# Conditioning products issued eight at a time in every fourth step, not four in every second

## The chip, the cores and the metric

The kernel runs on one core of one Trainium2 chip. The metric is the device time of one launch in microseconds. Before the change, three runs gave a median of 3303.23 us (3293.81 to 3304.52). One further execution was recorded by the profiler; it took 3296.7 us, of which 3294.9 us lie between its first and its last instruction. All durations below come from that execution.

## The reference

One inference step of a two-layer model on 256 prompt rows and 8 x 4 sample rows (288 columns in the kernel). Each layer has a mixer and a gated convolutional FFN, and each of them is modulated by six vectors that come from a small conditioning matrix:

```python
cond = jax.nn.silu(c.astype(F32)).astype(x.dtype)          # 9 rows: 8 samples and the prompt
for layer in range(DEPTH):                                 # 2
    mod = (cond @ p['w_ada'][layer] + p['b_ada'][layer])[:, None, :]
    sh1, sc1, g1, sh2, sc2, g2 = jnp.split(mod, 6, axis=-1)
    h = _rms(x, p['g_mix'][layer]) * (1 + sc1) + sh1
    y, ... = _mixer_ab(h, ...)   # or _mixer_cd in layer 1
    x = x + g1 * y
    h = _rms(x, p['g_ffn'][layer]) * (1 + sc2) + sh2
    y, fb = _conv_ffn(h, ...)
    x = x + g2 * y
```

`w_ada` is 2048 x 12288 in each layer, so each of the twelve vectors costs one product of 9 rows with a 2048 x 2048 float32 matrix (16 MB).

## The kernel before

**The large products.** `project` multiplies the activations with one weight matrix. It takes the weights in tiles of 128 x 1024 floats (512 KB, four blocks of 128 rows by 256 columns). `weights` loads one such tile (`raw`, line 175, on SyncE's queue), makes its rounded part `whi` on ScalarE (line 179) and the rest `wlo` on VectorE (line 180), and TensorE then runs 24 matrix products on it: for each of 8 blocks one on line 206 (`whi` with the high part of the activations), one on 207 and one on 208 (`wlo`). One weight tile with its 24 products is called a step here; there are 768 steps in the program.

**The conditioning products.** Two of the twelve vectors are made in the start phase by `ada_quarter`. The other ten are made by `ada_steps`, a generator that is advanced in the background: `Ctx.step`, called at the head of `weights`, resumes it once per step in both mixers (`every` is 1), about once in 1.9 steps in the first FFN and once in 2 steps in the second. It loads `w_ada` in tiles of the same size (`araw`, 128 rows by 1024 columns) and multiplies them with `cond` in `ada_groups` (line 1890). One block of 128 rows of `w_ada` needs two `araw` tiles and four products, which go to four different strips of 32 PSUM partitions. They are called a group of four here. The profile counts each of these float32 products as two instructions, so a group of four appears as x8.

**Buffers.** `raw` and `araw` share one pool of five buffers, `whi` and `wlo` have three each:

```python
class Ctx:
    raw_bufs, hl_bufs, kb = 5, 3, 4
    c.wraw = ctx.enter_context(tc.tile_pool(name="wraw", bufs=c.raw_bufs))
    c.whl = ctx.enter_context(tc.tile_pool(name="whl", bufs=c.hl_bufs))
```

A `raw` buffer is free again when VectorE has made `wlo`; an `araw` buffer when TensorE has run its two products. All `raw` and `araw` loads go through SyncE's queue in the order of the program, so a load that waits for its buffer holds up those behind it. The framework orders the instructions of each engine and gives out the buffers when the program is built; both are fixed in the built program.

Of the kernel before, what the change touches and what calls it, by code (L numbers as in the profile page):

```python
# [9 lines left out]
F32 = mybir.dt.float32  # L10
# [5 lines left out]
P = 128  # L16
# [5 lines left out]
D = 2048  # L22
KT = D // P
# [5 lines left out]
def bc(ap, axis, n):  # L29

    a = ap.unsqueeze(axis)
    s = list(a.shape)
    s[axis] = n
    return a.to_broadcast(s)
# [79 lines left out]
def mtile(c, name="pm"):  # L114
    return c.pm.tile([P, 512], F32, tag="pm", name=name)


def transpose(c, out, in_):
    n = in_.shape[0]
    b = in_.base_partition() if callable(getattr(in_, "base_partition", None)) else 0  # L120
    c.nc.tensor.transpose(out, in_, c.ident[:n, :n])  # L121
# [1765 lines left out]
def ada_groups(c, ps, cond, pieces, ks, first, last):  # L1887

    for r in range(4):
        c.nc.tensor.matmul(ps[32 * r:32 * r + 32, :], cond[:, ks[r], :], pieces[r], start=first, stop=last)  # L1890


def ada_steps(c, cond, w, which, bias, mod):

    nc = c.nc
    ps = c.pa.tile([P, 512], F32, tag="pa", name="pa")
    for k in range(KT):
        pieces = []
        for h in range(2):
            raw = c.wraw.tile([P, 1024], F32, tag="raw", name="araw")  # L1900
            nc.sync.dma_start(raw, w[k * P:(k + 1) * P, which * D + h * 1024:which * D + (h + 1) * 1024])
            pieces += [raw[:, 0:512], raw[:, 512:1024]]
            if h:
                ada_groups(c, ps, cond, pieces, [k] * 4, k == 0, k == KT - 1)
            yield
    pt = mtile(c)
    for t in range(0, 4, 2):
        sb = c.misc.tile([P, T], F32, tag="tmp", name="adas", bufs=2)[:, :2 * P]
        nc.scalar.copy(sb, ps[:, t * P:(t + 2) * P])
        for j in range(2):  # L1910
            transpose(c, pt[:, (t + j) * P:(t + j + 1) * P], sb[:, j * P:(j + 1) * P])
    pv = pt.rearrange("p (t j s) -> p j t s", t=4, j=4)
    mv = mod.rearrange("p (j t) s -> p j t s", t=4)
    bv = bias.rearrange("p (j t) -> p j t", t=4)
    for t in range(4):
        nc.vector.tensor_tensor(mv[:, :, t], pv[:, :, t, 0:9], bc(bv[:, :, t], 2, 9), ALU.add)
    yield
# [322 lines left out]
def trunk(tc, I, O):  # L2240
    nc = tc.nc
    with ExitStack() as ctx:
# [42 lines left out]
        with tc.tile_pool(name="start", bufs=1, side="right") as st:  # L2285
# [31 lines left out]
            for k in range(0, KT, 2):  # L2317
                act.scale(k)
            pr.place(c, slice(0, 1))
            ada = lambda l, i: ada_steps(c, cond, I["w_ada"][l], i, pr("b_ada%d" % l)[:, 16 * i:16 * i + 16], mods[l][:, i])  # L2320

            def quarter(q):
# [110 lines left out]
```

## Time and profile before

| what | value |
|---|---|
| median of three runs | 3303.23 us |
| the profiled execution, its span | 3296.7 us, 3294.9 us |
| TensorE busy with products | 3191.8 us, 97% |
| VectorE, ScalarE, GpSimd busy | 2060.3, 1451.5, 419.6 us |
| loads of `araw` and `raw` | 384 and 768, 512 KB each |
| conditioning products on line 1890 | 1536 instructions, 275.3 us |
| mean granted TensorE clock | 0.985 of full speed |

TensorE is busy nearly throughout, and the products overlap in its pipeline, so the busy times of single products (about 300 ns) are longer than the distance between their starts. What a piece of TensorE's work costs is read from start to start.

### The profile page before, as it was taken

Reading aid. Unit: us, or ns where it says so; the run is one execution under the profiler, and the core shown is the slowest. Engines: PE = TensorE matmul, PEld = TensorE weight load, DVE = VectorE, ACT = ScalarE, POOL = GpSimd, SP = SyncE. Lnnn points to the kernel's source line nnn. Section 1 sums busy time; section 2 is a strip of 40 time slices with the busy share of each in tenths; the row PEclk is TensorE's granted clock in tenths of the full one; section 3 lists DMA queues with packets and bytes.
Section 4 is the critical chain, followed back from the end, with each engine's and each line's share of the span. In section 5 each row is a group of like instructions: output and inputs, shape, how many; then the busy total and the mean of one; then the engine's idle time right before and its main releaser. Section 6 shows DMA issues by size and latency. Waiting matters only on the chain.

```text
span 3294.9 us, 58934 instructions
## 1 busy us (share of the span) xinstructions
PE 3191.8 (97%) x23220; PEld 2844.7 (86%) x23220; DVE 2060.3 (63%) x4291; ACT 1451.5 (44%) x2277; POOL 419.6 (13%) x786
## 2 busy tenths in 40 slices
PE   7899999999999999999999999999999999999998
PEld 3478888888889999999999977877889999999997
DVE  4255566676787566667656776666775556565566
ACT  1133343343554434343434675444464435444353
POOL 2000011110231101010001210112131101010020
PEclk9999999999999999999999999999999999999999
DMA  8866654545677777777777655665467755555553
GB/s 290 266 203 231 217 187 151 161 156 187 183 217 227 227 237 239 234 238 251 238 239 232 197 186 185 223 214 163 149 198 229 227 164 167 167 165 165 164 173 109
DMA packets 506615, 663.80 MB, mean 201 GB/s; under 512 B 42409, under 2 KB 436453, under 8 KB 506329
## 3 DMA queue, kind: packets, MB, share of 16 engines
q1 hardware_dynamic: 470930, 610.68, 58.5%
q0 software_dynamic: 14272, 40.76, 4.1%
q10 hardware_dynamic: 21136, 8.61, 1.0%
q8 instruction: 182, 2.98, 0.4%
q14 instruction: 95, 0.78, 0.1%
HBM read 634.13 MB, written 25.79 MB: 200 GB/s over the span
## 4 chain that ended last, share of the span: by engine, by line
PE 81%; DMA 9%; DVE 5%; ACT 3%; issue 2%; POOL 0%; SPq 0%; ACTq 0%; DVEq 0%; POOLq 0%
PE pp L206 22%; PE pp L208 22%; PE pp L207 22%; PE pa L1890 6%; DMA raw<-in_w_in_ab 3%; DVE wlo L180 2%; DMA araw<-in_w_ada 2%; DMA raw<-in_w_in_cd 2%; PE pm L121 1%; ACT whi L179 1%; PE pm L1100 1%; PE pm L1096 1%; PE pm L1104 1%; PE pm L1049 0%; PE pm L1827 0%
## 5 line engine op out<-in xcount | busy, mean ns | idle before, releaser
L206 PE MATMUL pp<-hhi,whi 128*128 128x288 f32 (+1 forms) x4736 | 1428.1, 302 | 6.9 <-ACT whi L179 3.3
L208 PE MATMUL pp<-hhi,wlo 128*128 128x288 f32 (+1 forms) x4736 | 1420.4, 300 | 8.8 <-DVE wlo L180 8.6
L207 PE MATMUL pp<-hlo,whi 128*128 128x288 f32 (+1 forms) x4736 | 1416.8, 299 | 0.1
L180 DVE TENSOR_TENSOR wlo<-raw,whi 128x1024 fp32r<-128x1024 f32 x768 | 943.3, 1229 | 753.3 <-ACT whi L179 737.7
L179 ACT CAST whi<-raw 128x1024 fp32r<-128x1024 f32 x768 | 805.4, 1049 | 1250.7 <-PE pp L207 723.7
L206 PEld LDWEIGHTS pp<-hhi,whi 128*128 128x128 f32 x4736 | 900.5, 190 | 138.8 <-issue 88.9
L208 PEld LDWEIGHTS pp<-hhi,wlo 128*128 128x128 f32 x4736 | 900.1, 190 | 35.3 <-DVE wlo L180 16.7
L207 PEld LDWEIGHTS pp<-hlo,whi 128*128 128x128 f32 x4736 | 899.8, 190 | 19.4 <-issue 15.5
L206 PE MATMUL pp<-hh,whi 128*128 128x288 f32 x1408 | 417.2, 296 | 0.0
L208 PE MATMUL pp<-hh,wlo 128*128 128x288 f32 x1408 | 416.7, 296 | 0.0
L207 PE MATMUL pp<-hl,whi 128*128 128x288 f32 x1408 | 413.5, 294 | 0.0
L1890 PE MATMUL pa<-araw,cond 128*32 128x512 f32 x1536 | 275.3, 612 | 21.7 <-DMA araw<-in_w_ada 21.7
L206 PEld LDWEIGHTS pp<-hh,whi 128*128 128x128 f32 x1408 | 264.7, 188 | 15.1 <-issue 13.4
L207 PEld LDWEIGHTS pp<-hl,whi 128*128 128x128 f32 x1408 | 266.6, 189 | 0.0
L208 PEld LDWEIGHTS pp<-hh,wlo 128*128 128x128 f32 x1408 | 264.2, 188 | 0.1
L507 DVE SCALAR_TENSOR_TENSOR cv<-pad,params,cv 128x304 f32<-128x304 f32 (+1 forms) x460 | 224.8, 532 | 20.1 <-ACT cv L505 11.8
L500 POOL COPY ffnpo<-pad 128x4 f32<-128x4 f32 x88 | 64.6, 734 | 1222.0 <-ACT pad L497 1222.0
L406 DVE SCALAR_TENSOR_TENSOR x<-pp,mod,x 128x256 f32<-128x256 f32 x256 | 112.4, 478 | 81.8 <-PE pp L208 80.8
L505 ACT ACTIVATE cv<-pad,params 128x304 f32<-128x304 f32 (+1 forms) x212 | 125.4, 637 | 7.8 <-DVE s_phi L1657 0.4
L1890 PEld LDWEIGHTS pa<-araw,cond 128*32 128x32 f32 x1536 | 39.7, 108 | 79.1 <-issue 40.4
L496 POOL COPY pad<-ffnsi 128x32 f32<-128x32 f32 x88 | 82.6, 938 | 18.1 <-ACT ffnsi L445 17.7
L497 ACT COPY pad<-pp 128x512 f32<-128x512 f32 x102 | 59.2, 581 | 12.9 <-PE pp L208 12.8
(785 smaller groups left out, 2618.0 us busy)
## 6 DMA issues: line engine op xcount, KB each, us to landing
araw<-in_w_ada SPq DMA_DIRECT2D x384, 512.0 KB, 4.8
raw<-in_w_ffn_up SPq DMA_DIRECT2D x352, 512.0 KB, 3.7
raw<-in_w_ffn_down SPq DMA_DIRECT2D x176, 512.0 KB, 3.5
raw<-in_w_in_ab SPq DMA_DIRECT2D x112, 512.0 KB, 4.9
raw<-in_w_in_cd SPq DMA_DIRECT2D x56, 512.0 KB, 5.1
raw<-in_w_out_ab SPq DMA_DIRECT2D x32, 512.0 KB, 5.5
raw<-in_w_out_cd SPq DMA_DIRECT2D x32, 512.0 KB, 3.6
s5d<-5p_D ACTq DMA_DIRECT2D x8, 838.0 KB, 5.6
```

The source lines that it names most:

```text
L179: nc.scalar.copy(hi[:, :n], raw[:, :n])
L180: nc.vector.tensor_tensor(lo[:, :n], raw[:, :n], hi[:, :n].bitcast(F32), ALU.subtract)
L206: nc.tensor.matmul(o, hi[:, k, js], ah, start=(k0 + k == first), stop=False)
L207: nc.tensor.matmul(o, hi[:, k, js], al, start=False, stop=False)
L208: nc.tensor.matmul(o, lo[:, k, js], ah, start=False, stop=(k0 + k == last))
L406: nc.vector.scalar_tensor_tensor(x[:, k + j, :SEQ], y[:, j, :SEQ], g[:, k + j, 8:9], x[:, k + j, :SEQ], ALU.mult, ALU.add)
L496: nc.gpsimd.tensor_copy(pv[:, :, :, 0:n], sv)
L497: nc.scalar.copy(pad[:, :, n:n + SEQ], ps[:, :, :SEQ])
L500: nc.gpsimd.tensor_copy(po[:, :, t0:t0 + 2], pad[:, :, SEQ:SEQ + n].rearrange("p j r -> p r j"))
L505: nc.scalar.activation(a, pad[:, j, 0:L], AF.Identity, scale=w(0), bias=pr(bname, t0 + j))
L507: nc.vector.scalar_tensor_tensor(a, pad[:, j, i:i + L], w(i), a, ALU.mult, ALU.add)
L1890: c.nc.tensor.matmul(ps[32 * r:32 * r + 32, :], cond[:, ks[r], :], pieces[r], start=first, stop=last)
```

## The change

`ada_steps` still gives way as many times, but it works in one resume out of four: it then loads four `araw` tiles (two blocks of 128 rows) one after the other and issues the eight products of both blocks together. Before, each resume loaded one tile, and every second one also issued four products. The number of loads and products is the same.

```diff
     ps = c.pa.tile([P, 512], F32, tag="pa", name="pa")
-    for k in range(KT):
+    for k0 in range(0, KT, 2):
+        for _ in range(3):
+            yield
         pieces = []
-        for h in range(2):
-            raw = c.wraw.tile([P, 1024], F32, tag="raw", name="araw")
-            nc.sync.dma_start(raw, w[k * P:(k + 1) * P, which * D + h * 1024:which * D + (h + 1) * 1024])
-            pieces += [raw[:, 0:512], raw[:, 512:1024]]
-            if h:
-                ada_groups(c, ps, cond, pieces, [k] * 4, k == 0, k == KT - 1)
-            yield
+        for k in (k0, k0 + 1):
+            for h in range(2):
+                raw = c.wraw.tile([P, 1024], F32, tag="raw", name="araw")
+                nc.sync.dma_start(raw, w[k * P:(k + 1) * P, which * D + h * 1024:which * D + (h + 1) * 1024])
+                pieces += [raw[:, 0:512], raw[:, 512:1024]]
+        for k in (k0, k0 + 1):
+            ada_groups(c, ps, cond, pieces[4 * (k - k0):4 * (k - k0) + 4], [k] * 4, k == 0, k == KT - 1)
+        yield
     pt = mtile(c)
```

In the built program TensorE's products of line 1890 stand in 229 unbroken runs before and in 153 now; of the latter 61 hold all eight products, the others are cut by small products of the mixers or belong to the start phase, which is the same in both.

TensorE in the first FFN, before: one run between two steps (`araw` is a tile of `w_ada`, `pp` the sum of a large product).

```order
L208 MATMUL pp_11506<-hh_8802,wlo_11552 128x288
L1890 MATMUL pa_11361<-araw_11507,cond_99 32x512 x2
L1890 MATMUL pa_11361<-araw_11585,cond_99 32x512 x2
L206 MATMUL pp_11584<-hh_8802,whi_11603 128x288
L207 MATMUL pp_11584<-hl_8803,whi_11603 128x288
```

The same place now:

```order
L208 MATMUL pp_11498<-hh_8802,wlo_11542 128x288
L1890 MATMUL pa_11361<-araw_11575,cond_99 32x512 x2
L1890 MATMUL pa_11361<-araw_11577,cond_99 32x512 x2
L1890 MATMUL pa_11361<-araw_11579,cond_99 32x512 x2
L1890 MATMUL pa_11361<-araw_11581,cond_99 32x512 x2
L206 MATMUL pp_11574<-hh_8802,whi_11603 128x288
```

Eight products stand together, and the next run of this kind comes seven or eight steps later, not four.

SyncE's queue at that place, before (a load that waits for `DVE` takes over the buffer of a weight tile, one that waits for `PE` that of a tile of `w_ada`; `DMAHW` are earlier loads):

```order
L1901 DMA araw_11507<-in_w_ada 128x1024 [waits DMAHW1_49,DVE_49]
L175 DMA raw_11509<-in_w_ffn_down 128x4x256 [waits DMAHW3_49,DVE_49]
L175 DMA raw_11549<-in_w_ffn_down 128x4x256 [waits DMAHW4_49,DVE_49]
L1901 DMA araw_11585<-in_w_ada 128x1024 [waits DMAHW0_49,PE_49]
L175 DMA raw_11601<-in_w_ffn_down 128x4x256 [waits DMAHW2_49,PE_49]
L175 DMA raw_11631<-in_w_ffn_down 128x4x256 [waits DMAHW6_49,DVE_49]
```

Now:

```order
L175 DMA raw_11539<-in_w_ffn_down 128x4x256 [waits DMAHW7_49,DVE_49]
L1904 DMA araw_11575<-in_w_ada 128x1024 [waits DMAHW0_49,DVE_49]
L1904 DMA araw_11577<-in_w_ada 128x1024 [waits DMAHW1_49,DVE_49]
L1904 DMA araw_11579<-in_w_ada 128x1024 [waits DMAHW2_49,DVE_49]
L1904 DMA araw_11581<-in_w_ada 128x1024 [waits DMAHW3_49,DVE_49]
L175 DMA raw_11601<-in_w_ffn_down 128x4x256 [waits DMAHW4_49,DVE_49]
L175 DMA raw_11631<-in_w_ffn_down 128x4x256 [waits DMAHW1_49,DVE_49]
L175 DMA raw_11677<-in_w_ffn_down 128x4x256 [waits DMAHW5_49,PE_49]
L175 DMA raw_11713<-in_w_ffn_down 128x4x256 [waits DMAHW6_49,PE_49]
L175 DMA raw_11749<-in_w_ffn_down 128x4x256 [waits DMAHW7_49,PE_49]
L175 DMA raw_11792<-in_w_ffn_down 128x4x256 [waits DMAHW0_49,PE_49]
```

The four `araw` tiles take four of the five buffers until their products have run. By the addresses in the built program, `raw_11601` takes over the buffer of `raw_11539`, the last weight tile ahead of the run of eight, and `raw_11631` takes over that of `raw_11601`.

SyncE's queue in the first mixer, where every step resumes `ada_steps`, now (before, one `araw` stood ahead of every `raw`):

```order
L1904 DMA araw_2478<-in_w_ada 128x1024 [waits DMAHW3_49,PE_49]
L1904 DMA araw_2480<-in_w_ada 128x1024 [waits DMAHW4_49,PE_49]
L1904 DMA araw_2482<-in_w_ada 128x1024 [waits DMAHW6_49,DVE_49]
L1904 DMA araw_2484<-in_w_ada 128x1024 [waits DMAHW7_49,DVE_49]
L175 DMA raw_2494<-in_w_in_ab 128x4x256 [waits DMAHW0_49,DVE_49]
L175 DMA raw_2537<-in_w_in_ab 128x4x256 [waits DMAHW5_49,DVE_49]
L175 DMA raw_2568<-in_w_in_ab 128x4x256 [waits DMAHW1_49,PE_49]
L175 DMA raw_2600<-in_w_in_ab 128x4x256 [waits DMAHW2_49,PE_49]
```

Here, too, `raw_2537` takes over the buffer of `raw_2494`, the load just ahead of it.

## Rows read from the trace of the kernel before

**Rows 1.** The page: busy time and share of the span by engine, the granted clock.

```profile
PE 3191.8 (97%) x23220; PEld 2844.7 (86%) x23220; DVE 2060.3 (63%) x4291; ACT 1451.5 (44%) x2277; POOL 419.6 (13%) x786
...
PEclk9999999999999999999999999999999999999999
```

**Rows 2.** The page: the chain that ended last, by engine.

```profile
PE 81%; DMA 9%; DVE 5%; ACT 3%; issue 2%; POOL 0%; SPq 0%; ACTq 0%; DVEq 0%; POOLq 0%
```

**Rows 3.** Timeline, one group of four in the first FFN: start us, us, engine.

```profile
1309.96 0.29 PE L208 MATMUL pp<-hhi,wlo 128*128 128x288 f32 x1
1310.18 0.16 PEld L1890 LDWEIGHTS pa<-araw,cond 128*32 128x32 f32 x8 [0.17 <-issue]
1310.19 1.06 PE L1890 MATMUL pa<-araw,cond 128*32 128x512 f32 x8
1311.18 0.40 PE L206 MATMUL pp<-hhi,whi 128*128 128x288 f32 x1
1311.42 0.29 PE L207 MATMUL pp<-hlo,whi 128*128 128x288 f32 x1
1311.55 0.29 PE L208 MATMUL pp<-hhi,wlo 128*128 128x288 f32 x1
...
1324.17 1.07 PE L1890 MATMUL pa<-araw,cond 128*32 128x512 f32 x8
```

**Rows 4.** Timeline, TensorE in the second mixer: five products in one run.

```profile
2187.59 0.29 PE L207 MATMUL pp<-hlo,whi 128*128 128x288 f32 x1
2187.82 1.90 PE L1890 MATMUL pa<-araw,cond 128*32 128x512 f32 x10
2189.65 1.13 PE L1424 MATMUL pm<-s_xw,s_Bt 128*128 128x512 f32 x2
```

**Rows 5.** Timeline, VectorE, SyncE's queue and ScalarE: from one buffer's release to its next.

```profile
1294.67 1.23 DVE L180 TENSOR_TENSOR wlo<-raw,whi 128x1024 fp32r<-128x1024 f32 x1 [1.12 <-ACT whi L179]
...
1295.93 0.37 SPq L175 DMA_DIRECT2D raw<-in_w_ffn_up  x1
...
1299.53 1.05 ACT L179 CAST whi<-raw 128x1024 fp32r<-128x1024 f32 x1 [3.18 <-DMA raw<-in_w_ffn_up]
...
1300.61 1.22 DVE L180 TENSOR_TENSOR wlo<-raw,whi 128x1024 fp32r<-128x1024 f32 x1 [3.01 <-ACT whi L179]
```

**Rows 6.** The same, where other ScalarE and VectorE work stands between.

```profile
1268.37 0.37 SPq L175 DMA_DIRECT2D raw<-in_w_ffn_up  x1
...
1272.06 1.05 ACT L179 CAST whi<-raw 128x1024 fp32r<-128x1024 f32 x1 [2.82 <-DVE cm_u L1507]
...
1273.77 1.22 DVE L180 TENSOR_TENSOR wlo<-raw,whi 128x1024 fp32r<-128x1024 f32 x1
```

**Rows 7.** Groups of line 179, second FFN without conditioning loads (2630:2900): busy, mean | idle, releaser.

```profile
L179 ACT CAST whi<-raw 128x1024 fp32r<-128x1024 f32 x84 | 88.4, 1052 | 136.2 <-PE pp L207 136.2
```

**Rows 8.** The same group in the first FFN (1150:1500).

```profile
L179 ACT CAST whi<-raw 128x1024 fp32r<-128x1024 f32 x99 | 103.7, 1048 | 176.4 <-PE pp L207 80.8 <-DMA raw<-in_w_ffn_up 56.2 <-DMA raw<-in_w_ffn_down 19.4
```

**Rows 9.** The same group in the first mixer (274:360).

```profile
L179 ACT CAST whi<-raw 128x1024 fp32r<-128x1024 f32 x21 | 22.0, 1049 | 54.0 <-DMA raw<-in_w_in_ab 54.0
```

**Rows 10.** Timeline, TensorE in the first mixer: starts of three groups of four (first halves).

```profile
275.38 0.64 PE L1890 MATMUL pa<-araw,cond 128*32 128x512 f32 x4
...
282.98 0.64 PE L1890 MATMUL pa<-araw,cond 128*32 128x512 f32 x4
...
290.54 0.64 PE L1890 MATMUL pa<-araw,cond 128*32 128x512 f32 x4
```

**Rows 11.** Stretches: us, busy (instructions) by engine, PEclk, DMA share and GB/s.

```profile
92.00:104.00 12.00, 10.35 (x49) 4.65 (x46) 2.07 (x6) 1.59 (x3) 0.00 (x0) 1.00 0.95 322
274.00:360.00 86.00, 83.80 (x621) 71.13 (x621) 33.15 (x44) 25.92 (x33) 3.58 (x6) 1.00 0.79 262
1150.00:1500.00 350.00, 349.78 (x2611) 324.40 (x2610) 236.58 (x570) 146.35 (x200) 32.30 (x68) 1.00 0.76 240
```

**Rows 12.** Weight loads of line 175 in 2630:2900, issue to landing.

```profile
DMA to landing us min/median/max: 3.3/3.6/5.5
```

**Rows 13.** The page: the groups of lines 206 and 208 in the large products.

```profile
L206 PE MATMUL pp<-hhi,whi 128*128 128x288 f32 (+1 forms) x4736 | 1428.1, 302 | 6.9 <-ACT whi L179 3.3
L208 PE MATMUL pp<-hhi,wlo 128*128 128x288 f32 (+1 forms) x4736 | 1420.4, 300 | 8.8 <-DVE wlo L180 8.6
```

## The prediction

> **What bounds the kernel now.** I read the page first. TensorE is busy for 97% of the span at nearly the full granted clock [rows 1], and 81% of the chain that ended last is TensorE's own work, with 9% DMA behind it [rows 2]. So there are two things to look for: what the change takes off TensorE's own time, and whether it makes weights arrive later than TensorE wants them.
>
> Next comes the price of a group of four, from start to start [rows 3]. The last large product ahead of it starts at 1309.96, the first one behind it at 1311.18, so 1.22 us pass. A plain step from one large product to the next is 0.13 us (1311.42 to 1311.55), and the first step behind the group takes 0.24. The group thus costs 1.22 + 0.24 - 2 x 0.13 = 1.20 us. The next group starts 13.98 us later [rows 3]; less 1.20 that leaves four steps of 3.20 us each, 24 products at 0.133. Nothing waits there.
>
> The third view is the way of one weight tile. Where a load waits for a buffer, it is issued at once when `wlo` of the old tile is done: VectorE ends at 1295.90, the load goes out at 1295.93, ScalarE starts at 1299.53, VectorE ends at 1301.83 [rows 5]. I call this a link: 5.9 us from issue to release. With other work in the way it took 6.6 us, from 1268.37 to 1274.99 [rows 6]. The load alone is about 3.6 us of it [rows 12], cast, subtraction and handing over 2.4 us.
>
> How early is a tile ready? In the second FFN without conditioning loads every idle time of line 179 ends with TensorE [rows 7]: the cast waits for one of three `whi` buffers, so it starts when TensorE is through with the tile three before. That is two steps, 6.4 us, ahead of its own use; 2.4 us later its `raw` buffer is free, **4.0 us ahead of its use**. In the first FFN 81 of 176 us idle end that way and 76 us with a load [rows 8]; in the first mixer all 54 us end with a load [rows 9]. So the lead is thinner where conditioning loads run, and thinnest in the mixers.
>
> **What the change takes away.** Two groups of four become one run of eight. The profile holds a run longer than four: five products (x10), where the fifth starts a second round on the strips [rows 4]. From the product ahead to the one behind it 2.06 us pass (2187.59 to 2189.65). A second round thus adds 2.06 - 1.20 = 0.86 us, not another 1.20; what is saved is one entry and one exit, 0.34 us. Built, the runs fall from 229 to 153, so 76 x 0.34 = **26 us** (0.8%) at most, all on TensorE, which is the bound.
>
> Here the Trainium skill speaks against the change. "TensorE: Matmul & The Clock Gate", section "Part 3: Packing small matmuls", says that weight loads overlap products in flight only when they use another group of rows. All products here use all rows, so by that rule the second four would wait for the first four to drain and nothing would be saved. The rows say otherwise: eight loads (two for each product) are over at 1310.34, while the products run to 1311.25 [rows 3], and the fifth product of [rows 4] did not cost another 1.20. I follow the rows.
>
> **What it adds: weights behind one buffer.** Instructions, bytes and resumes are the same. What moves is that four `araw` tiles now hold four of five buffers until their products have run, and the weight tiles behind them share what is left. By the built order the first two weight tiles behind the four loads go through one buffer, one after the other, and the rest wait in SyncE's queue behind the second of them.
>
> First FFN, 32 such runs. Call the last tile ahead of the run W0, then come the run, W1 and W2. W0's buffer is free 4.0 us ahead of its use. TensorE wants `wlo` of W2 after W0 (3.2), the run (2.06), W1 (3.2) and two products (0.27), 8.7 us after W0's first product. So 12.7 us are there for two links. Two clean ones take 11.8 and are just covered; two slow ones take 13.2 and cost 0.5 us; if W0 itself is a microsecond late, as ScalarE's and VectorE's other work in this stage makes likely now and then, it is 1.5. Bounds 0 and 1.5; I take 0.4, nearer the clean end since only some tiles meet such work: 32 x 0.4 = 13 us. A wait here moves TensorE as a whole; nothing else is late for it.
>
> Mixers, where each step resumes. A run now returns after four steps, and between runs eight tiles are loaded. Today two groups and four steps take 15.16 us (275.38 to 290.54) [rows 10]; with the saving, 14.8. The queue's own cycle is now: W2's load alone (3.6), behind it seven more loads, then cast and subtraction of the next W1 (2.4), whose buffer the next W2 needs. At 12 us of nearly full DMA use, 0.95 share gave 322 GB/s [rows 11], so a full rate of 339 and 1.55 us for 524,288 bytes. The cycle is 3.6 + 7 x 1.55 + 2.4 = 16.9 us against 14.8 on TensorE. Bounds 0 and 2.1 us a period; I take 1.5, near the upper end, for the chain has no slack of its own. It counts only where large products follow each other. Where 20 or more small products lie between two runs, the loads catch up. By the order there are eight periods with at most 14 small products that follow another such period, four in each mixer (in the second the buffers fall differently, but there a weight load waits for the run just ahead of it: it is ready 1.1 + 5.9 = 7.0 us after the run starts and wanted after 2.06 + 3.2 + 0.27 = 5.5, again 1.5). 8 x 1.5 = 12 us.
>
> Second FFN, eight runs: the same chain as in the first, without that stage's background work on ScalarE and VectorE. Covered by 12.7 against 11.8; nothing. If that cover went, 0.5 us each.
>
> **The sum.** -26 + 13 + 12 = -1 us: 3296.7 becomes about 3296 for the profiled execution. That one lay 6.5 us under the median of the runs; on the median I expect **3302 us**. About 0.3% (10 us) is what a measurement of this kernel can tell from no change.
>
> **Rivals.**
> *The loads are hidden after all: faster.* For it: DMA works at 0.76 to 0.79 [rows 11], TensorE loses nothing around the groups today, and small delays of ScalarE in the first FFN often fall where a tile is early. Then the first FFN costs nothing and the mixers half a microsecond a period, 8 x 0.5 = 4: -22 us, 3281. Against it: in the first mixer every cast already ends its idle time on a load [rows 9].
>
> *One buffer decides: slower.* The place is the first FFN, the load of W2 behind W1. It decides from the point where two links and the lateness of W0 together exceed 12.7 us in most runs, by more than 0.8 us on average (32 x 0.8 = 26 us, the whole gain). At 1.5 us there and 2.1 us in the mixers it is 48 + 17 - 26 = +39, 3342; halfway between that and my values about +20, 3322. For it: links of 6.6 us occur [rows 6], and 76 us of the 176 idle before casts in that stage end with a load even now [rows 8]. Against it: two clean links fit.
>
> *The change does not do what it says: no saving.* If eight in a run cost as two times four, by the mechanism of the rule above (its page is "TensorE: Matmul & The Clock Gate"), the 26 us fall away and the waits stay: +25, 3327. The second round of [rows 4] speaks against it.
>
> **Chances.** Gain and waits about cancel, 3302: 0.45. Hidden, faster: 0.24. One buffer, slower: 0.28. No saving, slower: 0.03. The range reaches from the first rival, 3281, to just short of the upper bound of the second: 3282 to 3332 leaves out about 1 in 10 at either end. The likeliest case alone is 3292 to 3312. Faster by over 0.3% 0.24, within 0.45, slower 0.31.
>
> **What would show it.** In the profile after, the timeline should have runs of eight (x16) that take about 2.06 us from the product ahead to the one behind. Around the second step behind a run in the first FFN, TensorE's line 208 should wait for VectorE's line 180 by 0 to 1 us, in some runs and not in others; the idle time ahead of lines 206 and 208 is 6.9 and 8.8 us in the whole span today [rows 13], and I expect some 25 us more there. In the mixers' pure stretches runs should start 16 us or more apart. The prediction is wrong if the second step behind a run is never late (then it is faster), if it is late by over a microsecond in most runs (slower), or if a run of eight takes 2.4 us.

## The result and the profile after

The changed kernel takes 3322.51 us (median of 5 runs, 3314.71 to 3324.14), against 3303.23 (3293.81 to 3305.76) before: a ratio of 1.006, 95% interval 1.0043 to 1.0077. It is slower by about 19 us. The prediction was 3302 and no change; the measured time lies 20 us above that, near 3322, the halfway value of the case called "one buffer decides"; that the two agree so closely is luck, for halfway means 0.95 us a run in the first FFN, and 0.77 was measured. The profiled execution took 3322.53 us, with a span of 3320.7 (before 3294.9).

The page of the changed kernel, the lines that answer to [rows 1, 2, 13]:

```profile
PE 3181.7 (96%) x23220; PEld 2860.4 (86%) x23220; DVE 2059.3 (62%) x4291; ACT 1451.5 (44%) x2277; POOL 407.5 (12%) x786
...
PEclk9899999999999999999999999999999999999999
...
PE 35%; DMA 2%; DVE 1%; ACT 1%; issue 1%; POOL 0%; DVEq 0%; ACTq 0%; POOLq 0%; SPq 0%
...
L206 PE MATMUL pp<-hhi,whi 128*128 128x288 f32 (+1 forms) x4736 | 1426.1, 301 | 24.3 <-ACT whi L179 19.5
L208 PE MATMUL pp<-hhi,wlo 128*128 128x288 f32 (+1 forms) x4736 | 1422.8, 300 | 20.4 <-DVE wlo L180 20.1
```

TensorE is busy 10 us less than before, as it should be with fewer switches between large and small products, but the span is 26 us longer. The idle time ahead of lines 206 and 208 went from 6.9 + 8.8 to 24.3 + 20.4 us: 29 us more, nearly all of it waiting for the cast (`whi`) or the subtraction (`wlo`) of a weight tile. (The chain of this page covers only 40% of the span, so its shares can't be set beside those of [rows 2].)

**The run of eight costs what was predicted.** TensorE's timeline in the first FFN (start us, us):

```profile
1276.44 0.29 PE L208 MATMUL pp<-hhi,wlo 128*128 128x288 f32 x1
1276.66 1.92 PE L1890 MATMUL pa<-araw,cond 128*32 128x512 f32 x16
1278.52 0.40 PE L206 MATMUL pp<-hhi,whi 128*128 128x288 f32 x1
1278.75 0.29 PE L207 MATMUL pp<-hlo,whi 128*128 128x288 f32 x1
```

From the product ahead to the one behind 2.08 us pass (predicted 2.06); two separate groups pass in 1.22 each [rows 3].

**The wait behind it is there too, and larger.** Another run in the first FFN. W0 is the last weight tile ahead of the run, W1 and W2 the next two, which share one `raw` buffer. ScalarE casts W0 and VectorE subtracts it (the line numbers are those of the kernel; 1506 to 1510 make the tables for the S5 part of the second mixer):

```profile
1294.89 1.05 ACT L179 CAST whi<-raw 128x1024 fp32r<-128x1024 f32 x1 [2.15 <-PE pp L207]
```

```profile
1296.94 0.29 DVE L1506 TENSOR_TENSOR cm_t<-5p_D,s_phi 128x128 f32<-128x128 f32 x1
1297.15 0.28 DVE L1507 TENSOR_TENSOR cm_u<-5p_D,s_phi 128x128 f32<-128x128 f32 x1
1297.47 0.23 DVE L1509 TENSOR_TENSOR 5p_D<-cm_t,cm_u 128x64 f32<-128x64 f32 x1
1297.61 0.22 DVE L1510 TENSOR_TENSOR 5p_D<-cm_t,cm_u 128x64 f32<-128x64 f32 x1
1297.75 1.22 DVE L180 TENSOR_TENSOR wlo<-raw,whi 128x1024 fp32r<-128x1024 f32 x1
```

The cast is over at 1295.94, but in VectorE's order the tables' instructions stand ahead of the subtraction, which starts 1.8 us later, at 1297.75. Only when it ends, at 1298.97, is the buffer free for W1. SyncE, ScalarE and VectorE from there on:

```profile
1298.99 13.67 SPq L175 DMA_DIRECT2D raw<-in_w_ffn_up  x7
...
1305.05 7.61 SPq L175 DMA_DIRECT2D raw<-in_w_ffn_up  x6
```

```profile
1302.72 1.05 ACT L179 CAST whi<-raw 128x1024 fp32r<-128x1024 f32 x1 [0.82 <-DMA raw<-in_w_ffn_up]
...
1309.96 1.04 ACT L179 CAST whi<-raw 128x1024 fp32r<-128x1024 f32 x1 [5.62 <-DMA raw<-in_w_ffn_up]
```

```profile
1303.80 1.23 DVE L180 TENSOR_TENSOR wlo<-raw,whi 128x1024 fp32r<-128x1024 f32 x1 [0.24 <-ACT whi L179]
...
1311.04 1.23 DVE L180 TENSOR_TENSOR wlo<-raw,whi 128x1024 fp32r<-128x1024 f32 x1 [2.78 <-ACT whi L179]
```

(The first of these lines merges seven loads; the second is the same queue from the second load on.) The first link, W1, ends at 1305.03; the second load goes out at once, at 1305.05, takes 4.9 us to its cast (1309.96), and W2 is through at 1312.27. And TensorE, at the end of W1 and the start of W2:

```profile
1309.54 0.29 PE L208 MATMUL pp<-hhi,wlo 128*128 128x288 f32 x1
1311.06 0.40 PE L206 MATMUL pp<-hhi,whi 128*128 128x288 f32 x1 [1.22 <-ACT whi L179]
1311.30 0.29 PE L207 MATMUL pp<-hlo,whi 128*128 128x288 f32 x1
1312.32 0.40 PE L208 MATMUL pp<-hhi,wlo 128*128 128x288 f32 x1 [0.73 <-DVE wlo L180]
```

It stops twice within three products, exactly at the second tile behind the run. The idle time shown (1.22, 0.73) is less than the loss: from 1309.54 to 1311.06 pass 1.52 us instead of 0.13, and the step after a stop takes 0.24 instead of 0.13, so a stop costs 0.28 us more than the row says.

### The profile page after: what moved, and what is told of

It is laid out like the page before. It is cut to its first block, busy times and chain, and to the rows that moved or that the text cites. A ratio compares the mean times of both kernels' runs of the same rounds, so it can differ in the third digit from the quotient of the medians.

```text
span 3320.7 us, 58980 instructions
## 1 busy us (share of the span) xinstructions
PE 3181.7 (96%) x23220; PEld 2860.4 (86%) x23220; DVE 2059.3 (62%) x4291; ACT 1451.5 (44%) x2277; POOL 407.5 (12%) x786
## 5 line engine op out<-in xcount | busy, mean ns | idle before, releaser
L206 PE MATMUL pp<-hhi,whi 128*128 128x288 f32 (+1 forms) x4736 | 1426.1, 301 | 24.3 <-ACT whi L179 19.5
L208 PE MATMUL pp<-hhi,wlo 128*128 128x288 f32 (+1 forms) x4736 | 1422.8, 300 | 20.4 <-DVE wlo L180 20.1
L180 DVE TENSOR_TENSOR wlo<-raw,whi 128x1024 fp32r<-128x1024 f32 x768 | 944.2, 1231 | 732.3 <-ACT whi L179 729.2
L1890 PE MATMUL pa<-araw,cond 128*32 128x512 f32 x1536 | 251.3, 609 | 17.5 <-DMA araw<-in_w_ada 17.4
L500 POOL COPY ffnpo<-pad 128x4 f32<-128x4 f32 x88 | 55.4, 630 | 1225.8 <-ACT pad L497 1216.2
```

Source lines behind the costliest of these rows:

```text
L180: nc.vector.tensor_tensor(lo[:, :n], raw[:, :n], hi[:, :n].bitcast(F32), ALU.subtract)
L206: nc.tensor.matmul(o, hi[:, k, js], ah, start=(k0 + k == first), stop=False)
L208: nc.tensor.matmul(o, lo[:, k, js], ah, start=False, stop=(k0 + k == last))
L500: nc.gpsimd.tensor_copy(po[:, :, t0:t0 + 2], pad[:, :, SEQ:SEQ + n].rearrange("p j r -> p r j"))
```

## The experiments

To split the time by stage, the table takes, from each kernel's profiled execution, the start of the first large product of weight tile 7, 144, 176, 384 and 512 (of 768 tiles in order of use) and gives the differences in us. Tiles 7 to 144 are the first mixer, 176 to 384 are 208 tiles of the first FFN with 27 runs of eight (54 groups of four), 384 to 512 the second mixer.

```
kernel                                           7-144   176-384   384-512
before                                           768.4     731.3     650.0
after                                            784.2     743.7     646.2
e1  sixth buffer, eight everywhere               782.8     723.0     636.1
e2  sixth buffer, fours                          772.0     730.6     649.0
e3  eight in the FFNs only                       773.1     747.4     640.4
e4  eight in the mixers only                     780.0     733.7     634.1
e5  eight, S5 tables after the FFN               780.3     723.4     (holds the tables)
e6  fours, S5 tables after the FFN               776.7     729.2     (holds the tables)
e9  sixth buffer, eight in the FFNs only         764.6     723.0     644.1
e10 half the conditioning loads, eights          754.6     722.7     620.8
e11 half the conditioning loads, fours           757.5     730.8     637.5
e12 sixth buffer, eight in FFN 1 and mixer 2     770.3     723.2     637.7
```

Kernels with the same code in a stage differ by up to 12 us in the mixers and by up to 3 us in the first FFN where nothing waits; differences in the mixers are read with that in mind.

Most of the scatter in the mixers goes with the clock that TensorE is granted. In these traces it is either full or half, and at half clock the step from one large product to the next takes 0.24 us, not 0.13. In the first mixer the six kernels with groups of four and all loads run 14 us (e9) to 38 us (e6) at half clock and take 764.6 to 776.7 us; with half of that time taken off they lie within 755 to 758 us. The four with runs of eight and all loads run 31 us (e5) to 41 us (the changed kernel) at half clock; with half of that taken off they lie within 763 to 765 us.

**A sixth buffer (e1) and its control (e2).** The last of the four conditioning tiles gets a buffer of its own while the first FFN runs:

```diff
-        with tc.tile_pool(name="s5prep", bufs=1, reuse_waits="tile") as tp:
+        with tc.tile_pool(name="arx", bufs=1) as c.arx, tc.tile_pool(name="s5prep", bufs=1, reuse_waits="tile") as tp:
...
-                raw = c.wraw.tile([P, 1024], F32, tag="raw", name="araw")
+                raw = ((c.arx if h and k > k0 else None) or c.wraw).tile([P, 1024], F32, tag="raw", name="araw")
```

> The changed kernel with a sixth buffer of 4 KB per partition while the first FFN runs: the last of the four conditioning tiles of a run goes there, so two of the five shared buffers are left for the weight tiles behind the run, not one. (To make room, the condition vectors are stored without padding columns and the FFN's conv state goes out through the buffers of its other temporaries.) Theory 'one buffer': the waits of the first FFN (about 26 us more than before between large products there) shrink to a few us and the saving of the runs is left, so some 20 to 25 us less than the changed kernel: about 3300 us. Rival 'bunched loads': what delays the weight tiles is that 2 MB go out at once ahead of them, whatever the buffers; then 3318 to 3325.

> Control: the kernel before with the same sixth buffer in the first FFN, used by every fourth conditioning tile, and the same two edits that make room. Both theories: TensorE hardly waits in that stage today, so 3300 to 3306 us. If it is faster by over 10 us, the sixth buffer or the edits help by themselves, and the first experiment must be read against this one.

Measured: e1 3286.41 us, 0.9965 of before (0.9951 to 0.9979); e2 3292.09 us, 0.999 (0.9976 to 1.0004). The groups of TensorE in the first FFN (tiles 176 to 384), first the changed kernel, then e1 (its lines are one higher; busy, mean ns | idle):

```profile
L206 PE MATMUL pp<-hhi,whi 128*128 128x288 f32 x1152 | 342.8, 298 | 4.6 <-ACT whi L179 4.6
L208 PE MATMUL pp<-hhi,wlo 128*128 128x288 f32 x1153 | 342.0, 297 | 5.4 <-DVE wlo L180 5.3
...
L206 PE MATMUL pp<-hh,whi 128*128 128x288 f32 x512 | 152.5, 298 | 1.6 <-ACT whi L179 1.6
L208 PE MATMUL pp<-hh,wlo 128*128 128x288 f32 x512 | 152.0, 297 | 2.5 <-DVE wlo L180 2.5
```

```profile
L209 PE MATMUL pp<-hhi,wlo 128*128 128x288 f32 x1153 | 342.1, 297 | 0.0
L207 PE MATMUL pp<-hhi,whi 128*128 128x288 f32 x1152 | 341.5, 296 | 0.0
...
L207 PE MATMUL pp<-hh,whi 128*128 128x288 f32 x512 | 152.5, 298 | 0.0
L209 PE MATMUL pp<-hh,wlo 128*128 128x288 f32 x512 | 151.8, 296 | 0.0
```

The four loads still go out together; with one more buffer every wait in this stage is gone, and the stage falls from 743.7 to 723.0 us. That is 20.7 us for 27 runs, 0.77 us each, and it is the price of the one buffer. What is left against before, 731.3 - 723.0 = 8.3 us, is the saving: 0.31 us a run (against e2, which has the same two edits, 7.6 us or 0.28). "Bunched loads" is out.

**By stage (e3, e4).** Runs of eight only for some of the conditioning parts, the old function for the rest:

```diff
-            ada = lambda l, i: ada_steps(c, ...)
+            ada = lambda l, i: (ada_eight if (l, i) in ((0, 5), (1, 1), (1, 0), (1, 2), (1, 5)) else ada_steps)(c, ...)
```

(e4 has `not in`.)

> Runs of eight in the two FFNs alone (40 of 76), groups of four in the mixers as before. Theory 'one buffer' as the trace of after splits it by stage (weight tiles start 17 us later over the first FFN, 1 us earlier over the second): 3303 + 16 = 3319 us. Rival 'the mixers cost it': the FFNs keep their 40 x 0.34 = 14 us, 3290.

> Runs of eight in the two mixers alone, groups of four in the FFNs as before. By the shifts in the trace of after (first mixer 17 us later, second 8 us earlier): 3303 + 9 = 3312 us. If the mixers' shift is only the scatter of where small products fall, 3295 to 3303; if the mixers cost the whole loss, 3320.

Measured: e3 3310.48 us, 1.0051 (1.0035 to 1.0067); e4 3295.77 us, 0.9999 (0.9987 to 1.0011). The loss is the first FFN's; in the mixers gain and waits cancel. The ratio of e3, times 3303, is 3320, near the expected 3319. For e4 the number by the shifts, 3312, was too high: the trace of after had put 17 us on the first mixer and given only 8 back in the second, and e4 has 11.6 us more in the first and 15.9 less in the second. Of these some 5 and 8 us go with the clock: e4 runs 34 us of the first mixer at half clock (before 24) and 10 us of the second (before 27).

**Why W0 is late (e5, e6).** The S5 tables, worked out beside the first FFN, are made behind it instead:

```diff
-            c.background(2, s5_tables(
+            c.background(math.inf, s5_tables(
...
-            c.pace(math.inf)
-            c.pace(1.5, 48)
```

> The changed kernel with the S5 tables, which VectorE and ScalarE otherwise work out beside the first FFN, made between the FFN and the second mixer (nothing is left out; it costs a serial stretch). To be read against the next run. Theory 'one buffer, late W0': the tile ahead of a run is ready 4.0 us ahead in the first FFN as in the second, two links of 5.9 us fit in 12.7, and TensorE's waits for weights in that stage fall from about 22 us to under 5; so this kernel is 5 to 14 us faster than the next one. Rival 'slow loads' (links long because the DMA engines are busy with 2 MB at once): waits stay near 20 us, and this one is 10 to 20 us slower than the next.

> Control: the kernel before with the S5 tables in the same later place. Both theories: no waits of TensorE for weights in the first FFN; slower than the kernel before by the length of the tables' stretch, estimated at 100 to 250 us from VectorE's busy time.

Measured: e5 3434.47 us (1.0406, 1.0391 to 1.0421) and e6 3442.07 us (1.0426, 1.0407 to 1.0445). The tables cost about 140 us when nothing hides them, but with the tables out of the way the median with runs of eight is 8 us under that with groups of four, where it had been 19 us above. The two intervals overlap a little; the stage of the FFN settles it, 723.4 us against 729.2, as with the sixth buffer, and 0.9 us of waiting is left in it:

```profile
L206 PE MATMUL pp<-hhi,whi 128*128 128x288 f32 x1152 | 342.0, 297 | 0.0
L208 PE MATMUL pp<-hhi,wlo 128*128 128x288 f32 x1153 | 341.6, 296 | 0.9 <-DVE wlo L180 0.9
```

The one buffer alone does little harm, then; it does so together with the tables' work.

**Held buffers without the saving (e7), and loads spread out (e8).** Two attempts to keep one half of the change. e7 (four loads together, the products as two fours):

```diff
-        for _ in range(3):
+        for _ in range(2):
             yield
...
         for k in (k0, k0 + 1):
             ada_groups(...)
-        yield
+            yield
```

e8 has the loads of the kernel before (one in each resume) and the eight products behind the fourth.

> Four loads go out together as in the changed kernel, but the eight products run as two groups of four, one resume apart. The cost of holding four buffers stays, the saving of the run of eight goes. If the two terms stand apart as the prediction has them: the changed kernel's 3322 + 26 = about 3345 us (3335 to 3350). If the run of eight by itself is what hurts (a longer hold of TensorE), it is near the kernel before, 3303.

> Runs of eight, but their four loads go out one by one in four resumes as in the kernel before. Theory 'one buffer': the first three tiles now hold their buffers for up to three resumes longer, more weight tiles go through one or two buffers, so at least as slow as the changed kernel, 3322 to 3350. Rival 'bunched loads': without the bunch the waits go and the saving is left, 3280 to 3295.

Measured: e7 3380.2 us, 1.0249 (1.0234 to 1.0265); e8 3391.9 us, 1.0276 (1.0262 to 1.029). Both are far above what was expected, and neither is the clean test it was meant to be: when the program was built, the groups were taken apart. In the first FFN e7 runs its 54 groups in 65 pieces and e8 its 27 runs in 41. A piece is dear, as this lone product in e7 shows (two records are one product):

```profile
1371.76 0.29 PE L207 MATMUL pp<-hl,whi 128*128 128x288 f32 x1
1371.98 1.04 PE L1890 MATMUL pa<-araw,cond 128*32 128x512 f32 x2
1372.96 0.40 PE L208 MATMUL pp<-hh,wlo 128*128 128x288 f32 x1
```

It takes 1.20 us from product to product, where a whole group of four takes 1.22 [rows 3]. For e7's stage this explains the size: 743.7 + 8.3 (saving gone) + 11 extra pieces x 1.2 = 765, measured 768.2. For e8 (789.8) 14 extra pieces give 760 by the same estimate. TensorE also idles 31 us ahead of lines 206 and 208 there (14 in the changed kernel) and runs 24 us at half clock (3 in the changed kernel), which is about the rest. What e8 does show is that the loads spread out, as built here, do not take the waits away; that the tiles loaded early hold their buffers longer is the likely reason, but no run shows it by itself.

**The saving by itself (e10, e11).** Each conditioning tile feeds two pieces of a group, so that a run of eight holds two buffers and a group of four one:

```diff
-            for h in range(2):
-                raw = ...
-                pieces += [raw[:, 0:512], raw[:, 512:1024]]
+            raw = ...
+            pieces += [raw[:, 0:512], raw[:, 512:1024]] * 2
```

> The gain term by itself: as the changed kernel, but each conditioning tile feeds two pieces of a group (the first half of each row block is never loaded, so half of the conditioning weights is left out). Two buffers are held by a run, not four, and half the bytes move. To be read against the next run. Prediction's term: 85 runs fewer than the next kernel (142 against 227 by the built order) x 0.34 = 29 us faster than it. If waits of any other kind come with a run of eight, less: under 15.

> Control: groups of four as in the kernel before, each fed by one conditioning tile used twice (the same half of the conditioning weights is left out). Somewhat faster than the kernel before for the shorter waits on conditioning loads, 3280 to 3303 us.

Measured: e10 3236.85 us, 0.9815 (0.9792 to 0.9838); e11 3269.07 us, 0.9918 (0.9901 to 0.9934), a little faster than expected. The difference is 32 us for 85 fewer runs, 0.38 us each (0.34 predicted), and 8.1 us in the stage of the FFN, 0.30 a run. The second figure is the firmer one: in the profiled executions 16.7 us of the difference lie in the second mixer, where stages scatter. In the FFN no wait of another kind comes with a run of eight: TensorE is busy without a gap in e10's stage.

**Put together (e9, e12).**

> The two findings put together: runs of eight in the FFNs alone, with the sixth buffer in the first FFN, groups of four in the mixers as before. 40 runs fewer at 0.34 us and no waits: 14 us below the kernel before with that buffer, so 0.995 to 0.997 of the kernel before. If runs of eight in the mixers were worth something after all, it is slower than the first experiment's kernel (0.9965); if they cost something, faster.

> Runs of eight only where the runs so far show a gain: in the first FFN with the sixth buffer (that stage 7 to 8 us shorter) and in the second mixer (about 10 us shorter in the three runs that have them there). Groups of four in the first mixer, where those runs are some 11 us longer, and in the second FFN. If these stage times add up: 0.992 to 0.995 of the kernel before. If the mixers' shifts are scatter of the order and not of the runs of eight, it is no better than the first experiment's kernel, 0.9965.

e9 has e1's buffer and e3's choice of parts; e12 has e1's buffer and eights for all parts but those of the first mixer and the second FFN. Measured: e9 3288.86 us, 0.9971 (0.9958 to 0.9985), at the edge of what was expected and not to be told from e1; e12 3280.45 us, 0.9939 (0.9922 to 0.9956). e12 beats both kernels: 20 us under before and some 40 under the changed one. Its interval just touches e1's, so what the choice of stages adds is less sure than the gain itself.

## Why the prediction was wrong, step by step

- **The saving.** Right. Predicted 0.34 us for each pair of groups that becomes one run; measured 0.31 in the first FFN (e1), 0.30 there and 0.38 over the whole program (e10 against e11). The working had a small slip: the 2.06 us of the longer run still hold what the 1.20 us of the group had taken off; like for like the same rows give 0.36. The rival "no saving" would have had e10 at e11's time; it is 32 us below. That rival followed the rule of the Trainium skill in "TensorE: Matmul & The Clock Gate", section "Part 3: Packing small matmuls". The 26 us were there to be had.
- **The first FFN: the step that failed.** The mechanism was right, the size was not. "32 x 0.4 = 13 us" was taken "nearer the clean end since only some tiles meet such work", with a lateness of W0 of "a microsecond". The price is 0.77 us a run, so for all 32 runs about 25 us where 13 stood. Of the 27 runs in the stage of the table, 17 do not wait in the trace of after: W0's buffer is free 4.02 us ahead of its use (predicted 4.0), the links take 6.07 and 5.93 on average, and 0.75 us are to spare. The other 10 wait: there W0 is ready 2.53 us ahead on average, once only 0.3, and the links take 6.58 and 6.33. Together that is 1.65 us more than there is room for. Set beside the same runs in e1, the three steps around the run take 2.0 us longer in these 10, 20.2 us in all, which is nearly the whole of the 20.7 that the sixth buffer took away. So W0 is late not by a microsecond now and then, but in 8 of 27 runs, by 1.9 us on average and by up to 3.7. In the other two of the 10 only the links are slow. The estimate had a slow pair of links at 0.5 us and a late W0 on top at 1.5 as the upper bound; in the run shown above both come together and cost more than that. e5 shows that the tables are the cause: without them W0's lead averages 3.99 us and the stage waits 0.9 us in all. The timeline shows their place in VectorE's order; e5 does not separate that from their ScalarE work and their transfers.
- **The mixers.** The prediction set 12 us of the saving against 12 us of waits here: the sum holds (e4: 0.9999, 4 us either way), the parts do not. Over the kernels with eights the first mixer averages 782 us against 771 with fours; the second is 7 us shorter with eights (638 against 646). So the first loses 11 us net where about nothing was expected, and the second gains 7; with half of the time at half clock taken off, 7 and 5 are left. In the first, the period from 269.35 to 284.17 takes 14.82 us, which is the time without any wait, while the chain of loads was priced at 16.9 and runs were to start 16 us or more apart. Behind the next run but one, at 301.86, TensorE does wait:

```profile
301.63 0.30 PE L208 MATMUL pp<-hhi,wlo 128*128 128x288 f32 x1
301.86 1.92 PE L1890 MATMUL pa<-araw,cond 128*32 128x512 f32 x16
305.44 0.40 PE L206 MATMUL pp<-hhi,whi 128*128 128x288 f32 x1 [1.65 <-ACT whi L179]
```

  Two more waits follow within 4 us, and from 308.2 on the granted clock is half (0.51 in this row, the third number from the end) for 6.9 us:

```profile
308.20:315.10 6.90, 5.77 (x22) 5.35 (x23) 5.70 (x12) 3.54 (x4) 0.30 (x1) 0.51 1.04 365
```

  e1, e4 and e5, which run eights here too, show the same fall at 304.9 to 311.7; none of the six kernels with fours does. The sum of the prediction had no term for the clock. Over the first mixer TensorE idles 10 to 11 us for casts and subtractions in each of the four kernels with eights, against 3 to 4 in the six with fours. With half the loads (e10, e11) the first mixer loses nothing, and in e10 it never idles for a cast or a subtraction there, so the waits there hang on the conditioning tiles; whether on the buffers that they hold or on their bytes no run here tells apart.
- **The second FFN.** Right: none of its runs waits, W0's lead is 3.97 us, and its tiles 528 to 632 take 342.7 us against 344.2.
- **The rivals.** "One buffer decides" named the place, the link of W2, and the point from which it tips the sum, 0.8 us a run on average; 0.77 was measured. It spoke against itself with "two clean links fit". They do, in 17 of 27 runs. The rows held the warning: 76 us of idle time before casts that end with a load [rows 8], and a slow link of 6.6 us [rows 6] next to a clean one, in which ScalarE waited for one of the tables' lines (1507) on VectorE. I took what delays a tile for the exception; it comes with 10 of 27 runs. The sign that was set for "slower", a tile late by over a microsecond in most runs, did not appear either: 8 of 27 runs lose more than a microsecond, and that is enough.
- **The range** (3282 to 3332) held the time, the chances (0.31 for slower) had the direction as the second likeliest. Of the 20 us between forecast and result the first FFN accounts for about 12 (25 instead of 13). The rest is not traced to one place. Part of it goes with the clock: the five runs of the changed kernel had a mean granted clock of 0.981 to 0.984, the profiled one of the kernel before 0.985. In the 31 runs of the kernel before that were measured beside e1, the time falls from 3306 us at 0.980 to about 3290 at 0.988, so 0.003 of clock is worth some 6 us, an estimate.

## What to carry to other kernels

When a change makes transfers hold more buffers, the average lead of the tiles says little: sort the tiles by lead, see what share of them is late and by how much, and charge the shortfall of each. A slack of 0.9 us is none where the first tile is 1.9 us late in 8 of 27 runs. And before a batching that saves time on the bound engine is given up, try one buffer more for just the stage that waits: here 4 KB per partition turned a loss of 0.6% into a gain of 0.35%, and choosing the stages as well made it 0.6%.

## What the runs showed of the hardware

- A lone small product between large ones takes TensorE 1.20 us from the product ahead to the one behind, nearly the same as four on the four column strips (1.22); eight take 2.08. Of a group's 1.20 us about 0.3 to 0.36 lie in going over to the small shape and back, which is what joining two groups saves; the rest is one round on the strips, and it costs the same with one product as with four. The Trainium skill, "TensorEngine Tiling (Array Packing)", section "Key Properties", says that a change of tiling mode drains TensorE. The saving is in keeping with that, though no run here measures a drain by itself. A built order that moves one product out of a group thus adds a whole 1.20 us, as in e7.
- In a run of eight, TensorE's weight loads for the later products go out while earlier ones are in flight, although all of them use all rows. In the run at 1304.50 of the changed kernel the first eight load at the start, and two more fours follow at 1304.95 and 1305.38, long before the products end:

```profile
1304.50 0.16 PEld L1890 LDWEIGHTS pa<-araw,cond 128*32 128x32 f32 x8 [0.16 <-issue]
1304.50 1.93 PE L1890 MATMUL pa<-araw,cond 128*32 128x512 f32 x16
...
1304.95 0.13 PEld L1890 LDWEIGHTS pa<-araw,cond 128*32 128x32 f32 x4 [0.30 <-issue]
...
1305.38 0.13 PEld L1890 LDWEIGHTS pa<-araw,cond 128*32 128x32 f32 x4 [0.30 <-issue]
```

- Conditioning loads cost time even in groups of four: with half of them gone (e11), the kernel is 27 us faster (0.9918). Against the average of the kernels with fours and all loads (771 and 646 us), 13 us of it lie in the first mixer and 8 in the second, and next to none (0.5 us against the kernel before) in the first FFN.
